# Moving the stores of the in-chunk systems and their inverses from ACT's DMA queue to SP's

## Chip, cores and metric

The kernel runs on one core of a Trainium2 chip. The metric is the device time of one execution in microseconds (us), lower is better. The number to compare with is the median of the runs shown below.

## What is computed

Two layers of a hybrid encoder trunk, in float32, over 1024 prompt tokens and 8 samples of 16 tokens. All branches of a layer read one projection of the normalised input:

```python
def trunk_layer(x, p, hist):
    z = rms_norm(x, p['norm_g']) @ p['w_in']
    ...
    ya, shift_n, wkv_n = rwkv7_mix(za, shift0, s0, p)     # A: delta-rule matrix state, per token
    yb, ckv, kr = mla_prompt(zb, p)                       # B: latent attention
    yd, pool_n = pool_mix(zd, None, p)                    # D: trailing means
    yc, vn = sgu_mix(zc, p)                               # C: spatial gating
    y = jnp.concatenate([ya, yb, yc, yd], axis=-1) * jax.nn.silu(gates)
    return x + y @ p['w_out'], ...
```

The change lies in branch A, whose per-token recurrence is

```python
def step(s, inp):
    r_t, w_t, k_t, v_t, kk_t, a_t = inp
    sa = jnp.einsum('bhij,bhj->bhi', s, -kk_t)
    s = s * w_t[:, :, None, :] + sa[:, :, :, None] * (kk_t * a_t)[:, :, None, :] + v_t[:, :, :, None] * k_t[:, :, None, :]
    return s, jnp.einsum('bhij,bhj->bhi', s, r_t)
```

## The kernel before

The tokens lie on the free axis, in three groups of 384. For each of 24 blocks of 128 output features, `project` (helper `mm`, L76) multiplies the weight block with the three groups, 24 matmuls of 128x384 for each group, into one of two PSUM buffers `pj`. A sink function then empties the buffer: ACT copies it (L383), DVE adds the token shift (L387 to L397), and small copies by ACT keep the last column (L386, L399, L400). The weights come in pieces by SP's queue (L238, three buffers `wr`); ACT rounds each (L241, `wh`), POOL subtracts (L242, `wl`), and only then is the `wr` buffer free for the next load.

Branch A runs as side work: its generators sit in a lane "a", and `tick()` inside `project` moves them on, so their instructions fall between the projection's.

- `a_elem` (L437 to L489, ACT and DVE in turn) makes the operands of one group.
- `systems` (L507 to L520) takes the 18 chunks of 64 tokens in turn: PE makes four 64x64 products, DVE masks them into a tile `ns` (L516), and a DMA on ACT's queue writes it to DRAM (`nd`, for the last two chunks `nds`; L517). `ns` has two buffers, so the mask of a chunk waits until the store of the chunk two before it has landed.
- `solve` (L522 to L555) loads all systems back in another layout by SP's queue (L530, L531) and inverts them by substitution on DVE, in pairs of instructions (L540, L542), first the small ones of the samples, then those of the prompt. The inverses go to DRAM by ACT's queue: two stores `dds` (L548), and four stores `dd` (L554, L555).
- `recurrence` takes the chunks 16, 17 (samples), then 0 to 15. `prepare` loads the inverse of a chunk by SP's queue (`tt`, L571 from `dds`, L573 from `dd`); for chunk 16, ACT copies the product of the samples' states (L612). `advance` multiplies with the inverse (ACT L664 empties the product), for the samples DVE masks the result four times (L668), and PE makes the new state from that.

By then `pool_gate` is being projected, whose sink is `silu` (ACT L758 to L760, DVE L761) and a product (DVE L822).

The order of instructions on each engine, and of the DMAs on each queue, is laid out when the program is built, by a planner that uses its own estimates of durations; it is not the order of the code (the load at L766 is in the code ahead of all of `systems`, and is issued in the middle of it). At run time each engine and queue goes through its list strictly in order. A DMA that an engine issues stands in that engine's list: its waits and its issue hold what is behind.

Of the kernel before, what the change touches and what calls it, by code (L numbers as in the profile page):

```python
# [48 lines left out]
def tile_trunk(ctx: ExitStack, tc: tile.TileContext, *aps):  # L49
# [23 lines left out]
    V, A, Po, PE, SY = nc.vector, nc.scalar, nc.gpsimd, nc.tensor, nc.sync  # L73

    def mm(out, lhsT, rhs, start=True, stop=True):
        return PE.matmul(out, lhsT=lhsT, rhs=rhs, start=start, stop=stop, skip_group_check=True)  # L76
# [10 lines left out]
    def nm(p):  # L87
        cnt[0] += 1
        return f"{p}_{cnt[0]}"
# [17 lines left out]
    def m_tile(cols=T):  # L107
        return mp.tile([128, cols], F32, tag="m", name=nm("m"))
# [10 lines left out]
    def pb():  # L119
        return ps_b.tile([128, 512], F32, tag="b", name=nm("b"))  # L120
# [201 lines left out]
    def halves(name, n, cols):  # L322
        return dr.tile([n, 128 * cols + 64], F32, tag=name, name=nm(name))

    def whole(t, c, cols):

        return t[2 * c:2 * c + 2, 0:128 * cols].rearrange("x (s t) -> x s t", s=64)

    def diagonal(t, i, n, cols, first=0):

        v = t[:, 0:128 * cols].rearrange("h (s i t) -> h s i t", s=64, i=2)[:, 0:n, i, first:first + n]
        step = n * (2 * cols + 1)
        assert v.ap[0][0] == step * (64 // n)
        return bass.AP(v.tensor, v.offset, [(step, t.shape[0] * 64 // n), v.ap[1], v.ap[2]])

    dd, dds = halves("dd", 32, 128), halves("dds", 4, 64)
    zer = m_tile(256)
    Po.memset(zer, 0.0)
    for x in range(2):
        z = zer[64 * x:64 * x + 64].unsqueeze(1)  # L340
        for t, n, cols in ((dd, 16, 128), (dds, 2, 64)):
            SY.dma_start(out=t[:, 0:128 * cols].rearrange("(c x) (s t) -> x s c t", x=2, s=64)[x],
                         in_=z[:, :, 0:2 * cols].broadcast_to([64, n, 2 * cols]))

    for l in range(L):
# [157 lines left out]
        nd, nds = halves(f"nd{l}", 32, 64), halves(f"nds{l}", 4, 64)  # L503

        def hp(h):
            return slice(64 * (h % 2), 64 * (h % 2) + 64)

        def systems(g):
            for cl in range(6):
                c = 6 * g + cl  # L510
                pn = pb()[:, 0:128].rearrange("p (i t) -> p i t", i=2)
                for h in range(4):
                    mm(pn[hp(h), h // 2, :], KB[h // 2][g][hp(h), cl, h % 2, :], AR[h // 2][g][hp(h), cl, 0, :])
                ns = chp.tile([128, 2, 64], F32, tag="u0", name=nm("ns"), bufs=2)
                mk = cm[:, C_MP if c < 16 else C_MS, 0:64]
                V.tensor_tensor(out=ns, in0=pn, in1=mk.unsqueeze(1).broadcast_to([128, 2, 64]), op=ALU.mult)  # L516
                A.dma_start(out=whole(nd, c, 64) if c < 16 else whole(nds, c - 16, 64),  # L517
                            in_=ns.rearrange("p i t -> p (i t)"))
                if cl % 2:
                    yield  # L520

        def solve():  # L522
            NT = m_tile(1024).rearrange("p (s t) -> p s t", s=32)
            DT = m_tile(1024).rearrange("p (s t) -> p s t", s=32)
            sol = m_tile(768)
            TM = sol[:, 0:256]
            NTs = sol[:, 256:512].rearrange("p (s t) -> p s t", s=16)
            DTs = sol[:, 512:768].rearrange("p (s t) -> p s t", s=16)
            for i in range(2):
                SY.dma_start(out=NT[64 * i:64 * i + 64], in_=diagonal(nd, i, 32, 64))  # L530
                SY.dma_start(out=NTs[16 * i:16 * i + 16], in_=diagonal(nds, i, 16, 64))  # L531

            def invert(NTt, DTt, n, np_):
                full = DTt[0:np_]
                Po.memset(full, 0.0)
                Po.memset(full.rearrange("p s t -> p (s t)")[:, 0:n * n:n + 1], 1.0)
                for s in range(n - 1):
                    w = n - 1 - s
                    tm = TM[0:np_, 0:(s + 1) * w].rearrange("p (j t) -> p j t", t=w)
                    V.tensor_tensor(out=tm, in0=full[:, 0:s + 1, s:s + 1].broadcast_to([np_, s + 1, w]),  # L540
                                    in1=NTt[0:np_, s:s + 1, s + 1:n].broadcast_to([np_, s + 1, w]), op=ALU.mult)
                    V.tensor_tensor(out=full[:, 0:s + 1, s + 1:n], in0=full[:, 0:s + 1, s + 1:n], in1=tm, op=ALU.add)  # L542
                    if s % 3 == 2:
                        yield

            yield from invert(NTs, DTs, 16, 32)
            for i in range(2):
                A.dma_start(out=diagonal(dds, i, 16, 64), in_=DTs[16 * i:16 * i + 16])  # L548
            yield
            yield from invert(NT, DT, 32, 128)  # L550
            DN = NT
            V.tensor_copy(out=DN, in_=DT.rearrange("p s t -> p t s"))
            for i in range(2):
                A.dma_start(out=diagonal(dd, i, 32, 128), in_=DT[64 * i:64 * i + 64])  # L554
                A.dma_start(out=diagonal(dd, i, 32, 128, 64), in_=DN[64 * i:64 * i + 64])  # L555


        Sst = {}
# [348 lines left out]
        def after_k1(g, zs):  # L907
            start("a", a_elem(1, g, zs))
            if g > 0:
                go("a", systems(g - 1))  # L910
# [4 lines left out]
        shifted(K1, lambda g: zk1[:, gcols(g)], after_k1)  # L915
        go("a", idle(4))
        go("a", systems(2))
        go("a", idle(4))
        go("a", solve())
        receptance(0, R0)  # L920
        receptance(1, R1)
# [683 lines left out]
```

## Time and profile before

| | |
|---|---|
| median of 3 runs | 1441.29 us (1440.91 to 1446.11) |
| the profiled execution | 1443.43 us, span 1441.6 us |
| PE (matmuls) busy | 1357.0 us, 94% of the span |
| DVE, ACT, POOL busy | 54%, 52%, 32% |
| SP's queue (weight and other loads) | 73.74 MB |
| ACT's queue (stores) | 21.94 MB |
| chain that ended last, by engine | PE 67%, DVE 17%, DMA 5%, ACT 4% |

A timeline row gives start, duration, engine, source line and operation, out<-in, the number of instructions merged, and in brackets the time for which the engine idled before it with the instruction that ended this. "ACTq" and "SPq" rows are DMA issues; they are not counted as busy. A busy PE is not a PE at its peak, because matmuls overlap and their ends are modelled.

### The profile page before, as it was taken

How to read it: one execution, taken by the hardware profiler on the slowest of the kernel's cores; microseconds unless marked ns; L12 is line 12 of the kernel's file. 1: busy time of each engine (PE TensorE's matmuls, PEld its weight loads, DVE VectorE, ACT ScalarE, POOL GpSimd, SP SyncE). 2: the span in 40 equal slices, each digit the busy share in tenths (PEclk: the TensorE clock that was granted, in tenths of full speed). 3: DMA queues.
4: the chain of work that ended last, by engine and by line, in shares of the span. 5: the costliest groups of instructions: out<-in, count | busy, mean ns of one | idle time of the engine just before them, and what ended most of it. 6: DMA issues, size and time to landing. Idle time of an engine off the chain costs nothing.

```text
span 1441.6 us, 26906 instructions
## 1 busy us (share of the span) xinstructions
PE 1357.0 (94%) x9962; PEld 1157.6 (80%) x9962; DVE 779.5 (54%) x1758; ACT 747.8 (52%) x2013; POOL 466.8 (32%) x600
## 2 busy tenths in 40 slices
PE   4799989999999998999989998999999999899999
PEld 3678878888988886679977788788789788766998
DVE  6875954435235567752287858444532375777211
ACT  6762234655466677652257621555653676766210
POOL 4514404426411023232162333332653111422320
PEclk9899999999999999999999999999999999999999
DMA  7212241210211213033300123321122111131222
GB/s 222 53 34 70 67 101 42 65 46 25 92 50 65 66 37 118 15 103 106 93 29 30 47 67 68 89 70 50 32 73 68 53 58 58 47 101 45 76 93 77
DMA packets 116596, 97.40 MB, mean 68 GB/s; under 512 B 46129, under 2 KB 111345, under 8 KB 116465
## 3 DMA queue, kind: packets, MB, share of 16 engines
q1 hardware_dynamic: 76776, 73.74, 17.8%
q10 hardware_dynamic: 39688, 21.94, 5.1%
q8 instruction: 79, 1.29, 0.4%
q14 instruction: 53, 0.43, 0.1%
HBM read 71.48 MB, written 24.16 MB: 66 GB/s over the span
## 4 chain that ended last, share of the span: by engine, by line
PE 67%; DVE 17%; DMA 5%; ACT 4%; issue 3%; POOL 3%; SPq 0%; ACTq 0%; DVEq 0%; POOLq 0%
PE pj L76 40%; PE b L76 14%; PE st L76 8%; DMA nd<-ns 3%; PE pj L1306 3%; DVE ea L278 2%; DVE m L540 2%; DVE m L542 2%; DMA tt<-dd 1%; POOL sp L99 1%; PE b L588 1%; DVE gn L730 1%; DVE ea L170 1%; DMA m<-nds 1%; DVE m L793 1%
## 5 line engine op out<-in xcount | busy, mean ns | idle before, releaser
L76 PE MATMUL pj<-xh,wh 128*128 128x384 f32 x1152 | 415.1, 361 | 19.3 <-ACT xh L280 7.3
L76 PE MATMUL pj<-xl,wh 128*128 128x384 f32 x1152 | 395.6, 343 | 3.8 <-POOL xl L282 2.8
L76 PE MATMUL pj<-xh,wl 128*128 128x384 f32 x1152 | 395.7, 344 | 0.0
L242 POOL TENSOR_TENSOR wl<-wr,wh 128x256 fp32r<-128x256 f32 x200 | 159.4, 805 | 459.6 <-ACT wh L241 398.0
L76 PEld LDWEIGHTS pj<-xh,wh 128*128 128x128 f32 x1152 | 220.9, 192 | 44.4 <-ACT sho L400 13.5
L76 PEld LDWEIGHTS pj<-xl,wh 128*128 128x128 f32 x1152 | 221.1, 192 | 12.1 <-POOL xl L282 4.8
L76 PEld LDWEIGHTS pj<-xh,wl 128*128 128x128 f32 x1152 | 220.6, 192 | 4.3 <-issue 3.1
L76 PE MATMUL pj<-yh,wh 128*128 128x384 f32 x384 | 129.3, 337 | 2.4 <-DVE x L1428 2.4
L76 PE MATMUL pj<-yh,wl 128*128 128x384 f32 x384 | 128.6, 335 | 0.0
L76 PE MATMUL pj<-yl,wh 128*128 128x384 f32 x384 | 128.3, 334 | 0.0
L241 ACT ACTIVATE wh<-wr 128x256 fp32r<-128x256 f32 x200 | 81.3, 414 | 80.7 <-PE pj L76 38.7
L242 POOL TENSOR_TENSOR wl<-m,wh 128x256 fp32r<-128x256 f32 x56 | 43.5, 789 | 102.8 <-ACT wh L241 84.9
L76 PEld LDWEIGHTS pj<-yh,wh 128*128 128x128 f32 x384 | 72.1, 188 | 3.7 <-DVE x L1428 2.7
L76 PEld LDWEIGHTS pj<-yl,wh 128*128 128x128 f32 x384 | 72.1, 188 | 0.1
L76 PEld LDWEIGHTS pj<-yh,wl 128*128 128x128 f32 x384 | 72.1, 188 | 0.1
L1295 ACT ACTIVATE X<-b,ng 128x512 f32<-128x512 f32 (+3 forms) x96 | 55.0, 577 | 25.6 <-DVE ng L1287 21.4
L76 PE MATMUL b<-sp,cr 128*128 128x384 f32 (+3 forms) x192 | 59.5, 385 | 3.2 <-POOL sp L99 2.8
L1283 DVE TENSOR_REDUCE mx<-b 128x1 f32<-128x512 f32 (+3 forms) x96 | 53.0, 555 | 9.7 <-PE b L76 8.0
L76 PEld LDWEIGHTS st<-X,X 128*64 128x64 f32 x576 | 35.1, 136 | 27.4 <-ACT X L1313 7.6
L1424 DVE TENSOR_TENSOR pt<-pj,pt 128x384 f32<-128x384 f32 x24 | 13.4, 557 | 80.6 <-PE pj L76 80.6
L241 ACT ACTIVATE wh<-m 128x256 fp32r<-128x256 f32 x56 | 22.2, 412 | 60.9 <-PE pj L76 59.2
L1306 PE MATMUL pj<-cm,X 128*128 128x128 f32 x288 | 48.0, 286 | 5.2 <-ACT X L1295 5.2
(307 smaller groups left out, 2584.9 us busy)
## 6 DMA issues: line engine op xcount, KB each, us to landing
wr<-in_win_dram SPq DMA_DIRECT2D x176, 128.0 KB
m<-in_wout_dram SPq DMA_DIRECT2D x12, 512.0 KB
x<-in_xT_dram SPq DMA_DIRECT2D x12, 384.0 KB
ysp<-m ACTq DMA_DIRECT2D x24, 192.0 KB
pt<-in_xT_dram SPq DMA_DIRECT2D x24, 192.0 KB
ea<-ysp SPq DMA_DIRECT2D x24, 192.0 KB
x1d<-x ACTq DMA_DIRECT2D x24, 192.0 KB
pt<-x1d SPq DMA_DIRECT2D x24, 192.0 KB
```

The source lines that it names most:

```text
L76: return PE.matmul(out, lhsT=lhsT, rhs=rhs, start=start, stop=stop, skip_group_check=True)
L99: by[1].tensor_tensor(out=view(lo), in0=src, in1=view(hi.bitcast(F32)), op=ALU.subtract)
L170: V.tensor_tensor(out=acc, in0=acc, in1=q, op=ALU.add)
L241: A.activation(out=h, in_=r, func=AF.Copy)
L242: Po.tensor_tensor(out=lo, in0=r, in1=h.bitcast(F32), op=ALU.subtract)
L278: V.scalar_tensor_tensor(out=t, in0=xs[k // 2][:, k % 2, :], scalar=vcs[:, l, V_NG + k:V_NG + k + 1], in1=rs, op0=ALU.mult, op1=ALU.mult)
L540: V.tensor_tensor(out=tm, in0=full[:, 0:s + 1, s:s + 1].broadcast_to([np_, s + 1, w]), in1=NTt[0:np_, s:s + 1, s + 1:n].broadcast_to([np_, ...
L542: V.tensor_tensor(out=full[:, 0:s + 1, s + 1:n], in0=full[:, 0:s + 1, s + 1:n], in1=tm, op=ALU.add)
L588: PE.transpose(pt[:, i * 128:(i + 1) * 128], KB[i][g][:, cl].rearrange("p a t -> p (a t)"), ident)
L1283: V.tensor_reduce(out=mx[:, b:b + 1], in_=pc[:, :w], axis=AX.X, op=ALU.max)
L1295: A.activation(out=P[:, :w], in_=pc[:, :w], func=AF.Exp, scale=SCALE, bias=ng, accum_out=sums[pr][:, b, s, h:h + 1])
L1306: PE.transpose(ptp[:, j * 128:(j + 1) * 128], Pb[slot][:, j * 128:(j + 1) * 128], ident)
```

## The change

The stores of `ns` (36 in the two layers), of `dds` (4) and of `dd` (8) are issued by SP (`SY`) in place of ACT (`A`). Nothing else is edited.

```diff
                 V.tensor_tensor(out=ns, in0=pn, in1=mk.unsqueeze(1).broadcast_to([128, 2, 64]), op=ALU.mult)
-                A.dma_start(out=whole(nd, c, 64) if c < 16 else whole(nds, c - 16, 64),
+                SY.dma_start(out=whole(nd, c, 64) if c < 16 else whole(nds, c - 16, 64),
                             in_=ns.rearrange("p i t -> p (i t)"))
...
             for i in range(2):
-                A.dma_start(out=diagonal(dds, i, 16, 64), in_=DTs[16 * i:16 * i + 16])
+                SY.dma_start(out=diagonal(dds, i, 16, 64), in_=DTs[16 * i:16 * i + 16])
             yield
             yield from invert(NT, DT, 32, 128)
             DN = NT
             V.tensor_copy(out=DN, in_=DT.rearrange("p s t -> p t s"))
             for i in range(2):
-                A.dma_start(out=diagonal(dd, i, 32, 128), in_=DT[64 * i:64 * i + 64])
-                A.dma_start(out=diagonal(dd, i, 32, 128, 64), in_=DN[64 * i:64 * i + 64])
+                SY.dma_start(out=diagonal(dd, i, 32, 128), in_=DT[64 * i:64 * i + 64])
+                SY.dma_start(out=diagonal(dd, i, 32, 128, 64), in_=DN[64 * i:64 * i + 64])
```

## Rows read from the trace of the kernel before

**Rows 1.** The chain that ended last, 84 to 240 us: start, us, what

```profile
98.28 4.75 DMA nd<-ns
...
128.16 3.09 DMA nd<-ns
...
131.69 3.77 DMA nds<-ns
...
136.51 4.86 DMA m<-nds
```

**Rows 2.** Busy time by stretch: us, PE, PEld, DVE, ACT, POOL, clock, DMA share

```profile
152.00:185.00 33.00, 28.33 (x215) 26.42 (x214) 31.47 (x77) 7.69 (x22) 14.58 (x20) 1.00 0.23 58
...
200.00:230.00 30.00, 29.76 (x393) 25.40 (x389) 14.85 (x30) 14.04 (x52) 12.14 (x17) 1.00 0.23 73
```

**Rows 3.** Instructions on the tiles nd and dd: ns min/median/max, and who waited

```profile
L517 ACTq DMA_DIRECT2D nd<-ns x32: 487/502/1090, 97.1 to 838.7; - x32
...
  DVE ns L516: 18.1, 17
...
L554 ACTq DMA_DIRECT2D dd<-m x4: 639/1510/2367, 186.0 to 897.5; - x4
L555 ACTq DMA_DIRECT2D dd<-m x4: 733/1102/1462, 187.1 to 899.9; - x4
```

**Rows 4.** Timeline of ACT, 92 to 140 us

```profile
107.81 0.53 ACT L455 ACTIVATE ea<-ea 128x384 f32<-128x384 f32 x1 [0.98 <-DVE ns L516]
...
123.05 4.09 ACTq L517 DMA_DIRECT2D nd<-ns  x3
...
133.89 0.42 ACT L241 ACTIVATE wh<-wr 128x256 fp32r<-128x256 f32 x1 [1.23 <-DMA wr<-in_win_dram]
```

**Rows 5.** Timeline of DVE, first layer and its twin in the second

```profile
108.36 0.62 DVE L468 SCALAR_TENSOR_TENSOR ea<-m,vcs,ea 128x384 f32<-128x384 f32 x1 [1.14 <-ACT ea L455]
...
128.91 0.62 DVE L387 SCALAR_TENSOR_TENSOR gn<-pj,vcs,gn 128x383 f32<-128x383 f32 x1 [0.66 <-ACT lc L386]
...
819.32 0.62 DVE L468 SCALAR_TENSOR_TENSOR ea<-m,vcs,ea 128x384 f32<-128x384 f32 x1 [1.14 <-ACT ea L455]
```

**Rows 6.** Timeline of SP's queue, 96 to 216 us

```profile
97.11 0.33 SPq L238 DMA_DIRECT2D wr<-in_win_dram  x1
...
131.34 0.33 SPq L238 DMA_DIRECT2D wr<-in_win_dram  x1
...
184.30 0.38 SPq L776 DMA_DIRECT2D zsm<-in_hist_dram  x1
195.82 0.51 SPq L573 DMA_DIRECT2D tt<-dd  x1
```

**Rows 7.** Timeline of POOL, 92 to 140 us

```profile
129.61 1.01 POOL L494 TENSOR_TENSOR ar<-gn,ar 128x384 f32<-128x384 f32 x1 [5.69 <-DVE gn L387]
130.58 0.74 POOL L242 TENSOR_TENSOR wl<-wr,wh 128x256 fp32r<-128x256 f32 x1
```

**Rows 8.** Timeline of ACT, 182 to 216 us

```profile
185.99 0.67 ACTq L554 DMA_DIRECT2D dd<-m  x1
...
191.89 0.66 ACT L612 ACTIVATE m<-b 128x256 f32<-128x256 f32 x2 [12.95 <-PE pj L76]
...
196.26 0.57 ACT L664 ACTIVATE vu<-b 64x128 f32<-64x128 f32 x2
```

**Rows 9.** Timeline of PE, 92 to 216 us, and one twin from the second layer

```profile
136.00 0.45 PE L76 MATMUL pj<-xh,wh 128*128 128x384 f32 x1 [1.96 <-ACT sho L400]
...
178.26 2.06 PE L76 MATMUL b<-ar,m 64*64 64x32 f32 x64
...
195.04 0.44 PE L76 MATMUL pj<-xh,wh 128*128 128x384 f32 x1 [0.56 <-DVE pt L761]
...
199.21 1.08 PE L76 MATMUL b<-m,kbt 128*64 128x256 f32 x8 [1.30 <-DVE m L668]
...
908.72 1.08 PE L76 MATMUL b<-m,kbt 128*64 128x256 f32 x8 [1.25 <-DVE m L668]
```

## Prediction

> **What bounds the kernel now.** I read the chain that ended last first, because the page's busy shares are means over stages. For most of the run the chain is PE's projection, but in each layer it leaves PE once, from about 98 to 186 us in the first layer and in the same way some 710 us later in the second. There it runs through branch A: stores of `ns`, the load of the small systems, then the substitution on DVE [rows 1]. Second, the busy time by stretch: from 152 to 185 us DVE is busy for 31.47 of 33 us, so DVE is the bound there and PE has slack; from 200 to 230 us PE is busy for 29.76 of 30, so PE is the bound and whatever is saved ahead of 200 us stays saved [rows 2]. Third, the two tiles that the change touches: DVE waited 17 times, 18.1 us in both layers, for a store of `ns` to land [rows 3]. Last, the timelines of ACT, SP, POOL, DVE and PE around these stores.
>
> **What is moved.** 36 stores of `ns` at a median of 0.502 us of issue, and eight of `dd` at 1.510 and 1.102 us (medians) leave ACT's list for SP's [rows 3]. The bytes, the transfers and DVE's work are the same. So the change can save only what waited behind a store in ACT's list, and can cost only what a store waits for in SP's list, or what waits behind it there.
>
> **Part one, the stores of the inverses.** The first `dd` store is issued at 185.99 us, when the substitution ends; the next thing that ACT does is L612, at 191.89 us, after 12.95 us without an instruction [rows 8]. The product that L612 copies was made by PE at 178.26 plus 2.06, so it was ready at 180.3 us [rows 9]. ACT thus stood for some 11.6 us in front of the stores, first waiting for the substitution, then issuing. Its backlog (L612, the silu of a gate, the copies for chunk 17) then runs one after the other, and the copy L664, on which DVE's masks depend, comes only at 196.26 us [rows 8]. PE waits twice behind this backlog: 0.56 us for a `pj` buffer that L761 frees, and 1.30 us for the masks L668; in the second layer the latter is 1.25 us [rows 9]. With the stores on SP, L612 and the first silu run before 186 us, in time in which ACT did nothing, and L664 comes earlier by about their length. I count all three waits as gone: 0.56 + 1.30 + 1.25 = 3.1 us. The bounds are 0, if something else is as late, and 3.1, since between these waits PE works in a fixed order and cannot go faster. I take 3.1, because the instructions that come out of the backlog are ready more than 10 us earlier.
>
> What do the stores cost on SP? Its queue issues nothing between 184.30 and 195.82 us, and at 195.82 comes the first load from `dd`, which needs the stores landed anyway [rows 6]. Four issues (two of 1.510, two of 1.102 us) are 5.2 us and fit into these 11.5 us. Cost: nothing. If that cover were gone, weight loads would start up to 5.2 us late, which only a PE out of weights would feel. The two `dds` stores of a layer I cost at nothing too: the load that follows them needs them landed in either order.
>
> **Part two, the stores of the systems.** From the tenth chunk on, DVE masks, the store is issued, it lands 3.09 us after its issue (4.75 and 3.77 us where a weight load is under way), and DVE may go on two chunks later [rows 1]. In that stretch ACT did not delay the stores, the stores delayed ACT: three in a row hold it for 4.09 us, most of it waiting for masks that were themselves waiting for earlier stores [rows 4]. SP cannot make a store land faster, so the pace stays. One place is different: ACT's L455 of the last group stood 0.98 us behind a store that waited for its mask [rows 4], and DVE, which has work lined up behind L468, idled 1.14 us for it, in both layers [rows 5]. From there DVE's work is dense up to the paced stretch, the paced stretch ends in the load of the small systems at 136.51 us [rows 1], and the substitution follows; so I count 2 x 1.14 = 2.3 us, with 0 and 2.3 as bounds.
>
> **What SP's list costs.** SP's list holds weight loads whose wait is for POOL. The load at 97.11 us stands just ahead of the first store, at 0.33 us of issue [rows 6]: I count 0.33 us for each layer, 0.7 us. The lower bound is nothing. The upper one is the load at 131.34 us: it waits for POOL's L242 at 130.58, that is behind L494 at 129.61, and this waits for DVE's L387 at 128.91 [rows 5 to 7]. If it were laid ahead of earlier stores, those would wait until 131.34. It cannot stand ahead of a store that DVE needs before L387, or the queues would wait for one another in a circle. The store issued at 128.16 [rows 1] had its mask done before L387, and that mask needed the store two chunks earlier. The earliest one that can be held is therefore the store between these two, which was the third in the row that begins at 123.05 and lasts 4.09 us [rows 4], so issued at about 126.6 us. Held to 131.34, that is 4.7 us in a layer. I take the lower end, since in ACT's own list the rounding that feeds this load stands behind these stores.
>
> [...] Here stores land in 3.09 us when alone and in 3.77 to 4.75 us near a weight load, on different queues [rows 1]. [...]
>
> **The sum.** -3.1 - 2.3 + 0.7 = -4.7 us. The profiled execution took 1443.43 us (span 1441.6), so it would take 1438.7; it lay 2.1 us above the median of 1441.29, so the median becomes 1436.6 us. A measurement tells 0.5% from no change here, 7.2 us; this forecast is inside.
>
> **Rivals.**
>
> *A larger gain.* PE waited 1.96 us at 136.00 for ACT's L400, the last step of emptying a `pj` buffer [rows 9], and ACT was late there because of stores and of roundings behind them. I count nothing for it, because PE's lead would be lost in the next 45 us, where DVE is the bound [rows 2]. But if the sinks then fall into the time in which DVE waits 4.86 us for the load of the small systems [rows 1], DVE has less to do later, and the wait is gained, in the second layer as much (an estimate from the first): -3.1 - 2.3 - 2 x 1.96 = -9.3 us, 1432.0. For it: DVE idles for that load. Against: the order is laid out anew and may not use it. Chance 0.25.
>
> *Slower: a load ahead of the stores on SP.* The load at 131.34 us holds the store by 4.7 us in each layer: 9.4 - 5.4 = +4.0 us, 1445.3. It is slower than before once it holds stores by more than 2.7 us in a layer, and visibly slower from (7.2 + 5.4) / 2 = 6.3 us, which needs held stores at more places than this. For it: all the loads in SP's list wait for POOL, at moments the planner only estimates. Against: the circle above. Chance 0.20, of which 0.12 above 0.5%.
>
> *Shared queue.* [...] Chance 0.10.
>
> *It does little.* The backlog is cleared earlier, but chunk 17 or the load from `dd` is next in line, so that only the 1.14 us of DVE remain, less 0.7: 1439.7. Chance 0.10.
>
> The forecast keeps 0.35.
>
> **Numbers.** Faster by over 0.5% is the larger gain and the fast edge of the forecast: 0.25 + 0.05 = 0.30. Slower by over 0.5% is 0.12 and 0.02 for the edges of the others: 0.14. Within 0.5%: 0.56. The range runs from 4 us under the larger gain, as an order laid out anew can also bring PE's later waits down, to 5 us above the slower rival, for a second held place: 1428 to 1450.
>
> **What would show it.** Part one: in the changed kernel ACT's L612 starts close to the end of its product, before the `dd` stores, and PE has no waits for L761 and L668 there. Part two: no wait of DVE's L468 for L455; the masks still wait for stores, about as long. SP: every store issued within 0.4 us of the end of its mask. It is wrong if stores stand behind weight loads on SP, if store landings grow over 4.75 us, or if the order on PE is another one altogether, so that the waits counted here have no counterpart.

## The result, and the profile after

The changed kernel takes 1436.77 us, the median of 15 runs (1433.73 to 1439.93), against 1444.73 us for 15 runs of the kernel before on the same chip. The ratio is 0.9947, with a 95% interval of 0.9934 to 0.9959: by this ratio 7.7 us less, between 5.9 and 9.5 us (the two medians differ by 8.0). The forecast was 4.7 us less. Sign and range hold; the size was too small, and it turns out below that the two halves of the sum were wrong in opposite directions.

The page of the changed kernel: the span, the busy time by engine, the two queues (packets, MB, share of 16 engines) and the chain by engine.

```profile
span 1436.9 us, 26896 instructions
...
PE 1358.3 (95%) x9962; PEld 1162.1 (81%) x9962; DVE 777.0 (54%) x1758; ACT 748.1 (52%) x2013; POOL 466.2 (32%) x600
...
q1 hardware_dynamic: 99056, 78.26, 19.5%
q10 hardware_dynamic: 17408, 17.42, 3.5%
...
PE 69%; DVE 16%; DMA 5%; ACT 3%; issue 3%; POOL 2%; SPq 0%; DVEq 0%; POOLq 0%; ACTq 0%
```

Against the kernel before, 4.52 MB moved from ACT's queue to SP's; the sum of the two is the same. PE has the same 9962 matmuls. Its idle time, span less busy, is 84.6 us before and 78.6 after: the two profiled executions, 4.7 us apart in their spans, show 6.0 us less idle time and 1.3 us more busy time. This split is rough. Another execution of the same changed kernel (below, "again") has 81.8 us of idle and 1353.7 us of busy time, and the granted clock differs between executions ahead of the first store that was edited (36 to 72 us: 0.88 of full speed before, 0.78 after).

The chain of the changed kernel from 84 to 240 us (start, us, what), and one line of the second layer's:

```profile
97.44 3.22 DMA nd<-ns
...
117.99 3.05 DMA nd<-ns
...
133.27 4.63 DMA m<-nds
...
193.46 5.78 DMA tt<-dd
...
224.31 5.99 DMA tt<-dd
...
901.65 5.68 DMA tt<-dd
```

Against [rows 1], three things differ. The first store on the chain lands in 3.22 us, where it took 4.75. The load of the small systems goes out at 133.27 instead of 136.51 us. And behind the substitution the chain now runs through the *first* load of an inverse from `dd`; before, the first such load on it was a later one:

```profile
229.38 6.64 DMA tt<-dd
```

The tiles `nd` and `dd` of the changed kernel (ns min/median/max, first and last start; then who waited, us and times):

```profile
L517 SPq DMA_DIRECT2D nd<-ns x32: 477/489/603, 94.3 to 832.7; - x32
...
  DVE ns L516: 14.6, 13
...
L554 SPq DMA_DIRECT2D dd<-m x4: 631/1486/2344, 182.7 to 891.9; - x4
L555 SPq DMA_DIRECT2D dd<-m x4: 812/1952/3380, 183.8 to 894.3; - x4
...
  PE b L76: 2.9, 4
```

DVE still waits for stores of `ns`, but 14.6 instead of 18.1 us [rows 3]. The second store of each pair of inverses issues more slowly on SP (median 1.952 us, 1.102 on ACT), and PE waits four times, 2.9 us, for inverses. Before it waited twice, 1.3 us.

### The profile page after: what moved, and what is told of

Read it like the earlier page. It is cut to its first block, busy times and chain, and to the rows that moved or that the text cites. A ratio compares the mean times of both kernels' runs of the same rounds, so it can differ in the third digit from the quotient of the medians.

```text
span 1436.9 us, 26896 instructions
## 1 busy us (share of the span) xinstructions
PE 1358.3 (95%) x9962; PEld 1162.1 (81%) x9962; DVE 777.0 (54%) x1758; ACT 748.1 (52%) x2013; POOL 466.2 (32%) x600
## 4 chain that ended last, share of the span: by engine, by line
PE 69%; DVE 16%; DMA 5%; ACT 3%; issue 3%; POOL 2%; SPq 0%; DVEq 0%; POOLq 0%; ACTq 0%
PE pj L76 41%; PE b L76 15%; PE st L76 9%; PE pj L1306 3%; DVE m L540 2%; DVE m L542 2%; DMA nd<-ns 2%; DVE ea L278 2%; DMA tt<-dd 2%; POOL sp L99 1%; PE b L588 1%; DVE gn L730 1%; DVE ea L170 1%; DVE kb L484 1%; DVE m L793 1%
## 5 line engine op out<-in xcount | busy, mean ns | idle before, releaser
L76 PEld LDWEIGHTS pj<-xh,wh 128*128 128x128 f32 x1152 | 221.6, 193 | 40.2 <-ACT sho L400 10.7
```

## Experiments

The texts on record name five theories. **A**: ACT's list held the first stores of `ns`, and releasing them is most of the gain. **B**: the prediction as it stood, most of it from the stores of the inverses. **C**: nearly all from the inverses. **D**, formed after the first runs: what moving the inverses' stores gains is given back to the wait for the load from `dd`. **E**, its rival: the waits that this move ends were never worth anything. Times saved are (1 - ratio) times the median of the runs of the kernel before that were timed beside the variant.

**The systems' stores alone.** On the kernel before, only L517 goes to SP; `dds` and `dd` stay on ACT.

```diff
-                A.dma_start(out=whole(nd, c, 64) if c < 16 else whole(nds, c - 16, 64),
+                SY.dma_start(out=whole(nd, c, 64) if c < 16 else whole(nds, c - 16, 64),
```

> Only the 36 stores of the systems (L517) are on SP's queue; the stores of the inverses stay on ACT's. Theory A (the stores of the systems carry over half of the gain, because ACT's list held the first ones back): 5 to 6 us under the kernel before, with the load of the small systems at about 133.3 us as in the changed kernel. Theory B (the sum on record): 2 x 1.14 - 0.7, about 1.6 us under it, that load at about 135.5. Theory C (the gain is the new order of PE behind the inverses): no difference of over 1 us.

1438.11 us, ratio 0.9958 (0.9946 to 0.997): 6.1 us saved. A's size, and its marker too: the load of the small systems at 133.01 us. C, no difference of over 1 us, falls.

**The inverses' stores alone**: L548, L554 and L555 on SP, L517 back on ACT.

> Only the stores of the inverses (dds, dd) are on SP's queue; those of the systems stay on ACT's. Theories A and B: 3 to 4 us under the kernel before, by the waits of 0.56, 1.30 and 1.25 us on PE that go; the load of the small systems stays at 136.5 us. Theory C: 7 to 8 us under it, all of the gain.

1443.25 us, ratio 1.0 (0.9982 to 1.0017). No difference, to 2.5 us either way, and every theory of that moment had expected one. The waits of PE, as they stood in the systems-only kernel (timeline of PE, 176 to 216 us; in brackets the idle time and its releaser):

```profile
188.70 0.45 PE L76 MATMUL b<-cm,m 64*64 64x64 f32 x8 [0.80 <-ACT m L612]
...
191.41 0.44 PE L76 MATMUL pj<-xh,wh 128*128 128x384 f32 x1 [0.65 <-DVE pt L761]
...
195.54 1.08 PE L76 MATMUL b<-m,kbt 128*64 128x256 f32 x8 [1.25 <-DVE m L668]
```

In the inverses-only kernel these three are gone (the prediction had named the last two), and one line stands in their place, with a twin of 1.35 us in the second layer:

```profile
200.56 0.43 PE L76 MATMUL b<-tt,gm 64*64 64x32 f32 x8 [1.74 <-DMA tt<-dd]
```

Right behind this wait, from 200 to 205 us, the granted clock is 0.66 of full speed. Behind the second layer's wait it stays at 1.00.

**The first two chunks' stores alone.** Only the stores of chunks 0 and 1 go to SP, four in the two layers.

```diff
-                A.dma_start(out=whole(nd, c, 64) if c < 16 else whole(nds, c - 16, 64),
+                (SY if c < 2 else A).dma_start(out=whole(nd, c, 64) if c < 16 else whole(nds, c - 16, 64),
```

> Only the stores of chunks 0 and 1 of the systems (4 of the 36 in two layers) go to SP's queue, all other stores stay on ACT's. Theory A (ACT's list holds just the first stores back, and the fourth mask waits for the second of them): the fourth mask starts at about 100.8 us in place of 103.1, and 3 to 4 us in all are gained. Theory B (what is gained is L455's wait behind later stores): no difference of over 1 us.

1438.92 us, ratio 0.997 (0.9958 to 0.9982): 4.3 us saved by four DMAs out of 48, where A had expected 3 to 4. The fourth mask came at 100.24 us (expected 100.8; 103.12 before), 7.0 us after the first one instead of 8.9.

**The changed kernel again**, beside these on the same chip.

> The changed kernel beside the three parts on one chip. By all theories 6 to 9.5 us under the kernel before. By A its gain is that of the systems alone plus that of the inverses alone, to 2 us.

1434.74 us, ratio 0.9944 (0.9932 to 0.9957): 8.1 us saved. The two parts alone saved 6.1 and 0, so this lies at the edge of the 2 us that A allowed.

**All but the first two.** The complement: chunks 0 and 1 stay on ACT, 2 to 17 go to SP: `(A if c < 2 else SY).dma_start(...)`.

> Complement of e3: the stores of chunks 0 and 1 of the systems stay on ACT's queue, those of chunks 2 to 17 go to SP's; the stores of the inverses stay on ACT's. If the first two stores carry about half of what the systems' stores bring (e3: 4.3 us of e1's 6.1, with 2.8 of 5.4 us of the stage from the first mask to the last load of the small systems), the other half is here: 1 to 4 us under the kernel before, that stage 1 to 1.5 us shorter in each layer. If the two parts are not separate (a late second store holds the later masks whoever issues those): no difference of over 1 us.

1445.61 us, ratio 1.0017 (1.0005 to 1.0028): 2.5 us *slower*, where a gain of 1 to 4 was expected. The lateness of the first stores is back. ACT's and the chain's rows of this kernel, in that order:

```profile
95.19 1.09 ACTq L517 DMA_DIRECT2D nd<-ns  x1
...
96.32 0.50 ACTq L517 DMA_DIRECT2D nd<-ns  x1
```

```profile
96.32 4.64 DMA nd<-ns
```

Two more things differ, as every variant gets its own order. On DVE (its timeline, 102 to 114 us) the mask of the seventh chunk stands behind the elementwise work of a group and starts at 110.32 us, 5.4 us after the sixth. Before, it started 2.0 us after it (106.97 and 108.99 us).

```profile
110.32 0.28 DVE L516 TENSOR_TENSOR ns<-b,cm 128x128 f32<-128x128 f32 x1
```

And on SP a weight load stands ahead of the store of the 17th chunk. SP's queue and then the chain:

```profile
129.34 0.33 SPq L238 DMA_DIRECT2D wr<-in_win_dram  x1
129.76 1.12 SPq L517 DMA_DIRECT2D nds<-ns  x2
```

```profile
130.40 4.75 DMA nds<-ns
```

The 17th mask ended at 128.73 us, so its store was held for 1.03 us (1.05 in the second layer). The last store, issued 0.64 us behind it, lands in 4.75 us (4.92), where in the changed kernel it takes 3.70 (3.80). The load of the small systems waits for it. This is the prediction's rival of a load ahead of the stores, and in this variant it came about.

So in this order the move of the later stores brings nothing; what it is worth by itself stays open. The parts don't add: -4.3 and +2.5 us against -6.1 for both, which the intervals (each about 1.7 us to either side) do not explain. By these rows, and not by a run, the held store is some 2 of the missing 4 us. DVE's new order is a candidate for the rest, not a shown cause.

**The granted clock** is a rival that no run here holds fixed. Its mean over the runs was 0.9884 for the first two chunks alone, 0.9870 for the systems alone and 0.9842 for the inverses alone, beside 0.9856 for the kernel before; it was 0.9848 for all but the first two, beside 0.9865. Among the runs of the kernel before, 0.001 of clock goes with 0.4 to 0.7 us (an estimate, the slopes in its three groups of runs). That would take 1 to 2 us from the 4.3 and some 1 us each from the 6.1 and the 2.5, and give the inverses alone up to 1 us. The changed kernel (0.9860) would lose 0.3 of its 8.1 us at most.

The length of the systems' stage, from the first mask (L516) to the second load of the small systems (L531), read from the timelines of DVE and SP:

| kernel | first layer, us | second layer, us |
|---|---|---|
| before | 42.26 | 41.82 |
| changed | 39.30 | 39.40 |
| systems only | 39.33 | 39.43 |
| first two chunks only | 41.06 | 40.24 |
| all but the first two | 43.96 | 43.67 |
| inverses only | 41.49 | 41.86 |

In the changed kernel the stage falls by 2.96 and 2.42 us in the two layers, 5.4 together. The substitution behind it is as long as ever (49.48 us before and after in the first layer).

**Theory D: the inverses' stores without the load from `dd`.** On the inverses-only kernel, and on the kernel before as a control, the operand `tt` is loaded from a weight block, which is there from the start.

```diff
-                SY.dma_start(out=tt.rearrange("p i t -> p (i t)"), in_=whole(dd, c, 128))
+                SY.dma_start(out=tt, in_=win[0, 0][:, 0:2, :])
```

> As e2 (only the stores of the inverses on SP's queue), but for chunks 0 to 15 the tile tt is loaded from the first weight block (same shape, rows of 1 KB) in place of dd, so that no load waits for the stores of the inverses; branch A's prompt output is therefore not that of the reference. Theory D (what the move of these stores saves at L612, L761 and L668 is lost again to the first load from dd, which lands 5.8 us after its issue, and to the slow clock behind that wait): 3 to 5 us under the control e9. Theory E (those waits on PE were never worth anything): within 1 us of e9.

> Control to e8: the kernel before (all stores on ACT's queue), with tt of chunks 0 to 15 loaded from the first weight block in place of dd; branch A's prompt output is not that of the reference. By both theories 0 to 2 us under the kernel before, for the two waits of 1.1 and 0.2 us for tt that its trace shows.

1437.89 us, ratio 0.9966 (0.9955 to 0.9978), with the stores moved, and 1441.38 us, 0.9991 (0.9982 to 0.9999), without. Once the load is out of the way, moving the stores of the inverses is worth 3.6 us, close to the 3.1 of the prediction's sum; with the load there it showed no worth. D holds and E falls. The edit takes away two things at once, though: the wait until the stores have landed, and the load itself, which is slow (5.6 to 6.0 us, below).

> The changed kernel, with tt of chunks 0 to 15 loaded from the first weight block in place of dd (same shape, rows of 1 KB), so that no load waits for the stores of the inverses; branch A's prompt output is not that of the reference. Theory D (the move of the inverses' stores is worth 3 to 4 us, lost to the load from dd): 10 to 12 us under the kernel before, 2 to 4 under the changed one. Theory E: at the changed kernel's time, 7.7 us under the kernel before.

The same edit on the changed kernel: 1429.92 us, ratio 0.9909 (0.9895 to 0.9923), 13.1 us saved, more than the 10 to 12 that D had expected (its mean clock is 0.9884, beside 0.9865: some 1 us by the estimate above). The loads from `dd` still cost the changed kernel some 5 us (13.1 less 7.7 to 8.1).

**More buffers for `ns`.** If the stores' landing sets the pace of the masks, six buffers in place of two should free it: `tag=("u0", "kbt", "vu")[c % 3]`, on the changed kernel and on the kernel before.

> The changed kernel with six buffers for ns in place of two (the tags u0, kbt and vu in turn, which are free in that stage). If the round trip of a store, 3.05 us and more for each two chunks, sets the pace from the tenth chunk on and the start of the substitution hangs on it: the load of the small systems at about 126 us in place of 133, and 8 to 15 us under the kernel before's time minus what the change itself brings, so 1420 to 1428 us. If the pace is set by PE or by the queue that issues the stores: no more than 2 us under the changed kernel.

> The kernel before with six buffers for ns, all stores on ACT's queue. If ACT's list, and not the two buffers, were what holds the stores, this gains nothing. By theory A (a mask waits for the store two chunks earlier, and that store waited in ACT's list): most of the gain of e4 is there too, since a late store then holds no mask: 8 to 16 us under the kernel before.

1438.19 us, 0.9966 (0.9954 to 0.9979), and 1441.21 us, 0.9987 (0.9978 to 0.9996). The gains of 8 us and more did not come. In the first kernel no mask waits for a store any more, and the small systems are loaded at 129.93 us, 3.3 us earlier than in the changed kernel, where 7 had been expected. The stores now stand behind one another: the DMA packets of the last six in the first layer run without a break from 119.35 to 128.44 us, 1.5 us for each store. So the stores themselves are the next limit, the other branch of that text. In the second kernel, A's expectation failed too: the stores are as late as ever in ACT's list (the first by 2.61 us, the sixth by 3.79).

The 3.3 us, too, gained nothing over the changed kernel. Part of the reason is visible in the first kernel's tile `dd` (who waited, us and times):

```profile
  PE b L76: 5.8, 4
```

The inverses are stored earlier, and PE then waits 5.8 us for loads from `dd`, in place of 2.9. PE's idle time over the whole span is 80.1 us, against 78.6 and 81.8 in the two executions of the changed kernel: a milestone of branch A had moved, and the idle time of the engine that bounds the kernel shows no gain.

**Why that load is slow.** It moves 128 KB in 5.6 to 6.0 us, as the chain of the changed kernel shows; its source `whole(dd, c, 128)` has an outer dimension of two. In the next kernel each load becomes two DMAs, one for each half of the partitions, with an outer dimension of 64.

```diff
+                for x in range(2):
+                    SY.dma_start(out=tt[64 * x:64 * x + 64].rearrange("p i t -> p (i t)"), in_=whole(dd, c, 128)[x])
```

> The changed kernel, with each load of tt from dd issued as two DMAs, one for each half of the partitions. If the 5.8 us of that load come from how one DMA with an outer dimension of 2 is spread (few DMA engines), each half lands in about 2.5 us, PE's wait for tt (2.9 us in four places) goes, and the time is 9 to 12 us under the kernel before. If they come from the stores just written or from the bytes, the load lands no earlier, SP issues 32 more DMAs, and the time is that of the changed kernel or up to 2 us more.

1433.57 us, ratio 0.993 (0.9917 to 0.9943): 10.1 us saved, inside the 9 to 12 expected, and some 2 us more than the change itself. The one load from `dd` that is left on the chain (230 to 330 us) is the second half of one, 2.27 us from its issue to its landing:

```profile
309.00 2.27 DMA tt<-dd
```

No wait of PE for `tt` is left in its trace. What sets a whole load apart from its halves shows in the traces. The kernel before issues 586 DMAs, whose semaphores are updated 8440 times: 16 times for each, but 3 times for each of the 72 whole stores of `ns` and loads of `tt` (514 x 16 + 72 x 3). With loads and stores in halves (the next kernel) 654 DMAs make 10412 updates, and only the 4 loads of `tt` from `dds`, which were not split, are left with 3. And the 128 packets of a whole store of `ns`, 28 ns each, go in 1.75 us, so two move at a time; the 64 packets of a half go in 0.3 to 0.4 us. Why that is so is not shown; that the outer dimension made the load slow rests on this split.

**The stores in halves too.** The stores of `ns` have the same outer dimension of two in DRAM, so they are split as well.

```diff
+                for x in range(2):
+                    SY.dma_start(out=(whole(nd, c, 64) if c < 16 else whole(nds, c - 16, 64))[x],
+                                 in_=ns[64 * x:64 * x + 64].rearrange("p i t -> p (i t)"))
```

> As e11, and each store of ns is issued as two DMAs too, one for each half of the partitions. If the spread counts for stores as well, the round trip of a store falls from 3.05 us to 2.0 to 2.5, and the stage of the systems is 2 to 4 us shorter in each layer; as six buffers for ns made that stage 2 us shorter and the kernel no faster, I expect at most 2 us under e11. If not, the extra issues of 0.5 us on SP make it 0 to 4 us slower than e11.

1429.03 us (1427.62 to 1429.36), ratio 0.9896 (0.9882 to 0.991): 15.0 us saved, about twice the change itself, and the fastest kernel of this study that computes everything. At most 2 us on top of the loads had been expected; it is 4.9. The stage had been expected 2 to 4 us shorter in each layer than in the kernel with the loads in halves; it is 0.1 and 1.2 us shorter (39.20 and 38.01 against 39.34 and 39.24), so this is 1.3 of the 4.9 us. From the load of the small systems to the first store of the inverses it takes 1.5 and 0.3 us less; the rest stays open. From its tile `nd` (issues; waits; landing):

```profile
L518 SPq DMA_DIRECT2D nd<-ns x64: 445/587/1698, 94.2 to 824.6; - x64
...
  DVE ns L516: 12.7, 11
...
DMA to landing us min/median/max: 1.7/1.9/3.6
```

A half lands 1.9 us after its issue, where a whole store took 3.05. The masks still wait (12.7 us), but no store of `ns` is on the chain from 88 to 240 us any more: PE's projection is. PE's idle time is 71.7 us, 12.9 less than before, which is more than the 3 us by which two executions of one kernel differ.

## Why the prediction was right in sign and wrong in its terms

**The bound** was read rightly: branch A through stores, systems and substitution, then PE. The substitution kept its length, and what changed did so in front of it and behind it.

**Part two is the term that was mis-sized**: 2.3 - 0.7 = 1.6 us in the sum, 6.1 us on the chip. The step that failed is "In that stretch ACT did not delay the stores, the stores delayed ACT". It holds from the tenth chunk on, for which it was written, and there a store lands on SP's queue about as fast as on ACT's (3.05 us at 117.99 us, 3.09 before [rows 1]); but the sum then used it for the whole stage. It is false for the first two stores, in the kernel before. DVE's masks there, and then ACT's rows with the stores of the first two:

```profile
94.25 0.28 DVE L516 TENSOR_TENSOR ns<-b,cm 128x128 f32<-128x128 f32 x1
...
97.42 0.28 DVE L516 TENSOR_TENSOR ns<-b,cm 128x128 f32<-128x128 f32 x1
...
103.12 0.29 DVE L516 TENSOR_TENSOR ns<-b,cm 128x128 f32<-128x128 f32 x1 [1.01 <-DMA nd<-ns]
```

```profile
96.58 0.53 ACT L457 ACTIVATE ar<-ea 128x384 f32<-128x384 f32 x1 [0.73 <-DVE ea L451]
...
97.15 1.09 ACTq L517 DMA_DIRECT2D nd<-ns  x1
...
98.28 0.50 ACTq L517 DMA_DIRECT2D nd<-ns  x1
```

The first mask ended at 94.53 us, and its store went out at 97.15: 2.6 us late, because ACT's list held it behind instructions such as L457, which itself waited 0.73 us for DVE. It then issued for 1.09 us, so that the second store, ready at 97.70, went out at 98.28 close behind it, and took 4.75 us to land. The fourth mask waited for that. The DMA packets in the trace tell why it took so long: those of the first store moved from 98.55 to 100.3 us, and those of the second directly behind them, from 100.3 to 102.2. In the second layer the first store is as late (2.62 us), and the second, issued at 809.00 us, again moves behind it, from 811.6 us. In the changed kernel (SP's queue, then DVE):

```profile
94.28 0.60 SPq L517 DMA_DIRECT2D nd<-ns  x1
96.83 0.33 SPq L238 DMA_DIRECT2D wr<-in_win_dram  x1
97.44 1.22 SPq L517 DMA_DIRECT2D nd<-ns  x2
```

```profile
97.87 0.28 DVE L516 TENSOR_TENSOR ns<-b,cm 128x128 f32<-128x128 f32 x1
...
100.78 0.29 DVE L516 TENSOR_TENSOR ns<-b,cm 128x128 f32<-128x128 f32 x1
...
128.17 0.29 DVE L516 TENSOR_TENSOR ns<-b,cm 128x128 f32<-128x128 f32 x1 [1.39 <-DMA nd<-ns]
```

The stores go out as their masks end, the third and fourth masks come 3.2 and 2.3 us earlier, and the last at 128.17 instead of 131.37 us. The rows were on the table: [rows 3] shows the issue of 1090 ns, with the first start at 97.1 us, and [rows 1] the landing of 4.75 us. I explained the 4.75 us by a weight load near it, where the packets show the first store, and never set the store's issue against the end of its mask.

**The wait for L455** behind a store is gone from DVE's rows, as forecast [rows 5]. It is gone from the first-two-chunks kernel too, where the later stores stay on ACT, so it does not hang on those stores alone; what its 2.3 us are worth within the 6.1 no run shows.

**Part one had the right waits and the wrong worth.** ACT's L612 starts at 179.36 us, not 191.89 [rows 8], 3.1 us after its product, and PE has no wait for L761 or L668. The prediction named 0 as its lower bound, "if something else is as late", and took the other end, because what comes out of the backlog is ready more than 10 us earlier. That is an argument about ACT alone. The something else is the load from `dd`. SP's queue after:

```profile
184.88 2.34 SPq L554 DMA_DIRECT2D dd<-m  x1
187.26 2.92 SPq L555 DMA_DIRECT2D dd<-m  x1
193.46 0.53 SPq L573 DMA_DIRECT2D tt<-dd  x1
```

From the substitution's end to that load it takes 10.7 us (182.75 to 193.46), against 9.8 before (185.99 to 195.82) [rows 6, 8]: the stores that were "cost: nothing" on SP issue more slowly there, and this path is 0.9 us longer. PE arrives earlier, and stands:

```profile
199.37 0.42 PE L76 MATMUL b<-tt,gm 64*64 64x32 f32 x8 [1.25 <-DMA tt<-dd]
```

That is the rival "it does little", to which I gave 0.10, for this half of the change. The waits themselves were counted a little short: PE also waited 0.30 us for L761 in the second layer and twice 0.24 us more for L668, 3.9 us in all, of which 3.6 were measured with the load out of the way.

Alone, the inverses' stores saved nothing, on top of the systems' some 2 us (8.1 less 6.1), a difference smaller than the two intervals.

**What SP's list costs** was sized at 0.33 us for a load laid ahead of the first store. The planner put that load behind it (96.83 us), and no store waited: it cost nothing. The slower rival, a load holding a store for 4.7 us, did not come about in the changed kernel: each of its 36 stores is issued 0.03 us after its mask. In the all-but-first-two kernel it did, with 1.03 us.

**The shared-queue rival**, a transfer kept behind that of a weight load on the same queue, fell. The store of 97.44 us is issued 0.6 us behind a weight load on the same queue and lands in 3.22 us, quicker than the 4.75 on another queue. Its packets do follow the load's directly (the load's last ends at 98.56 us, the store's first starts at 98.58). But it loses nothing by that here: it starts to move 1.14 us after its issue, the store of 94.28 us, with no load just ahead, 1.20 us. What does wait is a whole store close behind a whole store: those of 98.28 us before, of 96.32 and 130.40 us in the all-but-first-two kernel (4.75, 4.64 and 4.75 us), whose packets all run on without a break from the store ahead.

**The larger gain** came closer to the measured number (9.3 us), in part by its own mechanism. The wait for L400 that it counted, 1.96 us at 136.00 [rows 9] and 1.98 in the second layer, is gone from PE's rows. In its place PE waits 1.20 and 1.22 us for an earlier L400 (116.80 and 824.56 us), so 1.5 of its 3.9 us are left.

So 3.1 + 1.6 was forecast where the runs show 0 to 2 and 6.1: two errors that partly cancelled. That the total is only 3 us off, and inside the range, is in part luck; the 0.30 for faster by over 0.5% was low, with a result that lies just at that bound.

## What to carry to other kernels

To price a DMA in a compute engine's list, set each store's issue against the end of what it stores, the first ones above all: here, with two buffers, a first store 2.6 us late went with a last mask 3.2 us late (131.37 against 128.17 us). When a backlog is cleared, look at what arrives next at the same consumer (here a load, 5.8 us) before counting the wait as gained. And look at the outer dimension of every DMA on the chain: splitting two patterns took the 8 us that moving 48 stores between queues had saved here to 15.0. Two whole stores issued close together on one queue went one after the other, on ACT's queue as on SP's: the second landed in 4.75 us on each.

## What the hardware showed that I had not expected

- A 128 KB load with an outer dimension of two landed in 5.6 to 6.0 us; as two DMAs the second half landed 2.27 us after its issue. Stores of 64 KB: 3.05 us whole, 1.9 us for a half.
- The same store is not issued in the same time on the two queues: the last `dd` store of the first layer took 1.46 us on ACT and 2.92 us on SP.
- A store right behind a weight load on one queue was not slowed: 3.22 us, with the load issued 0.6 us ahead of it. A store 1.1 us behind another whole store was: 4.75 us, its packets directly behind the other's.
- In the kernel before, the 72 whole stores of `ns` and loads of `tt`, with an outer dimension of two, updated their semaphore 3 times each, the 514 other DMAs 16 times; the 128 packets of a whole store, 28 ns each, went in 1.75 us, two at a time.
